# w_ada sums on TensorE beside the first z half, triangular inverses from 16-blocks, last two token quarters begun with the FFN

## Chip, cores and metric

One core of a Trainium2 chip runs the program. The metric is device time in microseconds from launch to end; a measurement of this kernel tells differences of about 0.2% apart. The kernel is written in Bass and Tile: program order gives each instruction its priority, and the Tile scheduler, which plays the program through a model of the machine, fixes the order on every engine and on each DMA queue. An engine then runs its list strictly in that order, so an instruction that waits holds everything behind it. All DMAs named below but a few at the start are issued from SP's one queue.

## What is computed

```python
c_act = silu(c)
sh_m, sc_m, g_m, sh_f, sc_f, g_f = split(c_act @ w_ada + b_ada, 6)   # w_ada: 1024 x 6144
h = modulate(rms_norm(x), sh_m, sc_m)                                # x: 1024 x 1024
proj = h @ w_in                                                      # z: 1792 columns, u: 512
z = z + mu_shift * (shifted(z) - z)
y_rwkv = rwkv7_time_mix(z, ...)        # 8 heads x 64, a recurrence over 1024 tokens
y_s5 = s5_mix(u, ...)                  # 32 groups of a 64-wide complex diagonal state, then a GLU
x = x + g_m * (concat(y_rwkv, y_s5) @ w_out)
h = modulate(rms_norm(x), sh_f, sc_f)
x = x + g_f * ((silu(h @ w_gate) * (h @ w_up)) @ w_down)             # 2816 wide
return rms_norm(x) * final_gain
```

All in float32. The recurrence multiplies a 64 x 64 state per head by a decay and adds two rank-one terms per token.

## The kernel before

The tokens are taken in two halves of 512 for the projections and the FFN, and in four quarters of 256 for the recurrence. Every large product is three passes of float32r matmuls on operands split in a high and a low part (`mm3`, L266; `split`, L129): the high part is a ScalarE copy, the low part a subtraction on GpSimd or VectorE.

**The adaptive vectors.** `ada_load` (L280) fetches 128*n columns of w_ada for all 1024 rows in four DMAs. `ada_acc` (L289) multiplies the eight row blocks by the columns of `cact` and adds them up, 128 partial sums per column left on the partitions: one VectorE instruction per block (L295, L297), or a ScalarE product (L299) and a GpSimd sum (L300). `ada_cols` (L303) sums over the partitions with one matmul per 128 columns (`pac`, L306). Parts 0 and 1 are needed before anything is projected and are done at the start, four column blocks at a time. Parts 2 and 3 run beside `chains(0)` and `chains(1)` (`ada_steps`, L826, woven in L1251 and L1417), parts 4 and 5 beside the first output projection (L1428).

**The start** (to L592): x is loaded, normed, transposed and modulated to hT, u = h @ w_in is formed (`u_mm`, L365, tile `pu`), and the small S5 parameters are worked out on VectorE.

**The z halves.** `zblock` (L857, tile `pz`) forms 128 columns of z for 512 tokens with 24 matmuls, mixes in the shifted z and writes to `zt_d`. In the first half each weight block is loaded from w_in, split, and spilled as split to `zw_d` (`z_w`, L526); in the second it is read back. `zhalf(0)` is woven with the S5 units (L1224), `zhalf(1)` with the first two quarters.

**A quarter.** `prepare` (L1152) reads z from `zt_d` with eight DMAs and forms decays, keys and bonuses in 12 steps for each of two head groups (`prep`, L888; matmuls `pw`, `pa`, `pn`, `pb`). `post` (L1162) forms the chunk matrices `ak`, writes their strictly lower parts to `l_d`, and calls `solve` and `rest`. `solve` (L991) inverts the diagonal blocks of the 64-token triangles: it reads 32 x 32 blocks with the right-hand side's columns spread over the partitions, and substitutes in 31 steps of a product (L1006) and a sum (L1008), on VectorE for quarters 0 and 1 and on GpSimd for 2 and 3. The result and its transpose go through `x_d`. `rest` (L1013) joins two 32-inverses to one of 64 with 32 x 32 matmuls (`pG`, `pO`). `chains` (L1085) runs the four chunks of the recurrence, four steps each, and `finishes` (L1186) norms and gates the output into `y_d`.

**The order** is written out from L1220 on with `weave` (round robin over generators, with a number of steps each), `LIM` (only so many steps) and `alongside`. Around the change:

```python
1224  weave((zhalf(0), 2), LIM(s5g, 14))
1251  weave(c0, (LIM(glg, 18), 2), LIM(adg, 12))
1417  weave(LIM(c1, 14), finishes(0), (glg, 1), (adg, 3))
1425  weave(seq(c1, finishes(1)), LIM(o0, 4), LIM(late, 4))
1429  weave((LIM(late, 16), 2), o0, (LIM(adl, 2), 1))
1442  alongside(late, f0, 2)
1450  weave(LIM(f0, 28))
1451  weave((f0, 1), seq(outproj(1, ...), norm_f(1, ...)))
```

`late` (L1421) is quarters 2 and 3, 128 steps. `o0` is the output projection of the first half (`outproj`, L1282, tile `po`), 18 steps. `f0` (L1441) is the norm and the FFN of the first half, 97 steps; `alongside` (L1211) gives it one step for every two of `late`. Matmuls of the FFN are `pgate`, `pup` and `pdn`. The first 20 steps of `late` come before `f0` begins; of `f0`, 54 steps go with the rest of `late`, 28 alone, and 15 are left to run beside the second output projection.

## Time and profile before

| | |
|---|---|
| runs shown, median (lowest to highest) | 1596.32 us (1594.2 to 1597.29) |
| the profiled execution | 1596.48 us, span 1594.8 us |
| TensorE busy | 1419.0 us, 89% |
| VectorE busy | 929.3 us, 58% |
| ScalarE busy | 562.7 us, 35% |
| GpSimd busy | 519.8 us, 33% |
| mean granted TensorE clock | 0.946 of 2.4 GHz |
| moved by DMA | 211.8 MB, 133 GB/s over the span |

The busy share of the whole span says little here, since the stages have different limits. The windows of the trace cut the span by stage: the start (to 104 us), the first z half (to 226 us), the second with quarters 0 and 1 (to 444 us), the remaining chains with the GLU and the first output projection (to 670 us), the FFN of the first half with quarters 2 and 3 (to 1106 us), the second output projection and norm (to 1240 us), the FFN of the second half. For each engine a window has the busy time and in brackets the number of instructions; matmuls are pipelined, so their busy time contains waits inside a burst. The granted clock is given as a share of 2.4 GHz; its two levels are 1.2 and 2.4 GHz. The chain of waits goes back from the end of a stretch, at each step to what released it last.

### The profile page before, as it was taken

How to read it: one execution, taken by the hardware profiler on the slowest of the kernel's cores; microseconds unless marked ns; L12 is line 12 of the kernel's file. 1: busy time of each engine (PE TensorE's matmuls, PEld its weight loads, DVE VectorE, ACT ScalarE, POOL GpSimd, SP SyncE). 2: the span in 40 equal slices, each digit the busy share in tenths (PEclk: the TensorE clock that was granted, in tenths of full speed). 3: DMA queues.
4: the chain of work that ended last, by engine and by line, in shares of the span. 5: the costliest groups of instructions: out<-in, count | busy, mean ns of one | idle time of the engine just before them, and what ended most of it. 6: DMA issues, size and time to landing. Idle time of an engine off the chain costs nothing.

```text
span 1594.8 us, 23226 instructions
## 1 busy us (share of the span) xinstructions
PE 1419.0 (89%) x9167; PEld 1143.2 (72%) x9167; DVE 929.3 (58%) x1618; ACT 562.7 (35%) x909; POOL 519.8 (33%) x480
## 2 busy tenths in 40 slices
PE   3897888988968847989999998999997999999997
PEld 3675666776856535777777776778886888888885
DVE  5968328688656899464467655446356533333335
ACT  4442244443345632242145223224444222222223
POOL 4358333222143415163000007000611244444543
PEclk9998899899979869899999999899998999999999
DMA  9447895563664477244233243315621423232331
GB/s 286 139 139 244 264 328 193 164 163 110 154 160 125 126 219 217 59 103 97 61 99 91 88 106 89 84 54 167 177 80 40 151 87 106 92 106 92 98 101 53
DMA packets 255692, 211.80 MB, mean 133 GB/s; under 512 B 71894, under 2 KB 223072, under 8 KB 252000
## 3 DMA queue, kind: packets, MB, share of 16 engines
q1 hardware_dynamic: 254096, 208.67, 44.0%
q8 instruction: 72, 1.18, 0.3%
q0 software_dynamic: 816, 0.57, 0.2%
q10 hardware_dynamic: 672, 1.08, 0.2%
q14 instruction: 36, 0.29, 0.1%
HBM read 166.54 MB, written 45.84 MB: 133 GB/s over the span
## 4 chain that ended last, share of the span: by engine, by line
PE 51%; DVE 19%; DMA 13%; POOL 5%; ACT 5%; issue 4%; SPq 2%; DVEq 0%; ACTq 0%; POOLq 0%
PE pdn L270 11%; PE pgate L270 10%; PE pup L270 10%; PE pz L270 5%; PE po L1314 4%; DMA wada<-in_w_ada_dram 3%; PE pu L367 2%; DMA rawd<-in_ffn_w_down_dram 2%; PE p L1062 2%; DVE acc L297 2%; POOL stmp L1006 2%; POOL XU L1008 2%; PE pY L762 1%; PE pA L962 1%; DMA LU<-l_d 1%
## 5 line engine op out<-in xcount | busy, mean ns | idle before, releaser
L270 PE MATMUL pdn<-wd,act 128*128 128x512 f32 x1056 | 271.7, 398 | 1.4 <-DVE x L1363 0.5
L270 PE MATMUL pup<-h,hl_up 128*128 128x512 f32 x1056 | 266.5, 395 | 0.2 <-ACT hl_up L131 0.2
L270 PE MATMUL pgate<-h,hl_g 128*128 128x512 f32 x1056 | 262.7, 394 | 2.1 <-ACT hl_g L131 2.0
L270 PEld LDWEIGHTS pdn<-wd,act 128*128 128x128 f32 x1056 | 197.3, 189 | 49.1 <-DVE x L1363 2.4
L270 PEld LDWEIGHTS pgate<-h,hl_g 128*128 128x128 f32 x1056 | 196.6, 188 | 47.2 <-issue 3.2
L270 PEld LDWEIGHTS pup<-h,hl_up 128*128 128x128 f32 x1056 | 197.5, 188 | 43.9 <-issue 2.1
L270 PE MATMUL pz<-hT,hl_z 128*128 128x256 f32 (+1 forms) x1008 | 192.6, 347 | 35.0 <-ACT zo L872 13.5
L1363 DVE TENSOR_TENSOR x<-pdn,x 128x512 f32<-128x512 f32 x176 | 118.8, 688 | 176.6 <-PE pdn L270 176.4
L270 PEld LDWEIGHTS pz<-hT,hl_z 128*128 128x128 f32 x1008 | 159.0, 206 | 64.8 <-ACT zo L872 18.2
L1398 DVE TENSOR_TENSOR rawd<-rawd,gfb 128x1024 f32<-128x1024 f32 x44 | 57.2, 1300 | 111.5 <-DMA rawd<-in_ffn_w_down_dram 89.9
L1314 PE MATMUL po<-wo,yhl 128*128 128x512 f32 x384 | 98.7, 410 | 9.0 <-ACT yhl L1299 4.2
L1314 PEld LDWEIGHTS po<-wo,yhl 128*128 128x128 f32 x384 | 74.4, 197 | 27.3 <-ACT yhl L1299 4.3
L131 ACT CAST wd<-rawd 128x1024 fp32r<-128x1024 f32 x44 | 45.6, 1051 | 122.1 <-DVE rawd L1398 88.8
L131 ACT CAST hl_up<-raw_up 128x1024 fp32r<-128x1024 f32 x44 | 46.2, 1051 | 114.6 <-PE pup L270 105.1
L297 DVE SCALAR_TENSOR_TENSOR acc<-wada,cact,acc 128x256 f32<-128x256 f32 (+1 forms) x112 | 79.0, 710 | 6.9 <-DMA wada<-in_w_ada_dram 5.3
L875 POOL TENSOR_TENSOR zo<-zo,zm 128x512 f32<-128x512 f32 x28 | 44.2, 1580 | 99.5 <-ACT zo L872 86.6
L127 POOL TENSOR_TENSOR hl_g<-raw_g,hl_g 128x1024 fp32r<-128x1024 f32 x19 | 45.5, 2394 | 78.7 <-ACT hl_g L131 78.7
L127 POOL TENSOR_TENSOR yhl<-yt,yhl 128x512 fp32r<-128x512 f32 x16 | 25.0, 1562 | 135.5 <-ACT yhl L1299 130.9
L1392 ACT ACTIVATE sgt<-pgate 128x512 f32<-128x512 f32 x44 | 26.3, 599 | 121.0 <-PE pgate L270 120.0
L127 POOL TENSOR_TENSOR wd<-rawd,wd 128x1024 fp32r<-128x1024 f32 x19 | 49.7, 2616 | 57.4 <-ACT wd L131 57.4
L127 POOL TENSOR_TENSOR wo<-wraw,wo 128x512 fp32r<-128x512 f32 x32 | 44.4, 1393 | 73.6 <-ACT wo L131 73.6
L127 POOL TENSOR_TENSOR hl_up<-raw_up,hl_up 128x1024 fp32r<-128x1024 f32 x19 | 49.9, 2628 | 50.0 <-ACT hl_up L131 50.0
(373 smaller groups left out, 2345.5 us busy)
## 6 DMA issues: line engine op xcount, KB each, us to landing
raw_g<-in_ffn_w_gate_dram SPq DMA_DIRECT2D x44, 512.0 KB, 4.0
raw_up<-in_ffn_w_up_dram SPq DMA_DIRECT2D x44, 512.0 KB, 3.9
rawd<-in_ffn_w_down_dram SPq DMA_DIRECT2D x44, 512.0 KB, 3.6
wada<-in_w_ada_dram SPq DMA_DIRECT2D x64, 256.0 KB, 3.2
zw_d<-hl_z SPq DMA_DIRECT2D x14, 1024.0 KB
hl_z<-zw_d SPq DMA_DIRECT2D x14, 1024.0 KB, 4.9
wada<-in_w_ada_dram SPq DMA_DIRECT2D x16, 512.0 KB, 7.8
wraw<-in_w_out_dram SPq DMA_DIRECT2D x32, 256.0 KB, 4.4
```

The costliest lines, as they stand in the source:

```text
L127: (eng or G).tensor_tensor(out=out, in0=a, in1=b, op=ALU.subtract)
L131: S.copy(dst[:, 0], src)
L270: PE.matmul(ps, lhsT=lf(a, k), rhs=rf(b, k), start=(n == 0), stop=(n == 3 * kb - 1))
L297: V.scalar_tensor_tensor(out=acc, in0=wt, scalar=cact[:, k:k + 1], in1=acc, op0=ALU.mult, op1=ALU.add)
L367: PE.matmul(pu[hf, b], lhsT=uw[b][:, a_, k, :], rhs=hT[hf, k][:, b_, :], start=(k == 0 and n == 0), stop=(k == 7 and n == 2))
L875: G.tensor_tensor(out=o, in0=o, in1=zm[:, 0:HT], op=ALU.add)
L1006: SOLVE.tensor_tensor(out=t, in0=LU[:, j, j + 1:32].unsqueeze(2).to_broadcast([P, nt, nk]), in1=X[:, j:j + 1, 0:nk].to_broadcast([P, nt, n ...
L1008: SOLVE.tensor_tensor(out=X[:, j + 1:32, 0:nk], in0=X[:, j + 1:32, 0:nk], in1=t, op=ALU.add)
L1062: PE.matmul(ps[r, h], lhsT=a, rhs=b, start=(n == 0), stop=(n == len(ops) - 1))
L1314: PE.matmul(pss[i], lhsT=yh[k][:, a, 128 * i:128 * i + 128], rhs=wo[:, b], start=(k == 4 and n == 0), stop=(k == 3 and n == 2))
L1363: V.tensor_tensor(out=t, in0=ps, in1=t, op=ALU.add)
L1398: V.tensor_tensor(out=raw, in0=raw, in1=gfb, op=ALU.mult)
```

## The change

1. `ada_acc` multiplies on TensorE. `cz` holds each column of `cact` in a block of 32 columns of which the other 31 are zero; the eight row blocks are eight float32 matmuls with 32 weight columns each, spread over four column groups of the array (`tile_position`), two row blocks accumulated in each. ScalarE copies the four times 32 rows from PSUM, and `ada_cols` sums them as before.
2. `ada_steps` runs all of parts 2 to 5 beside `zhalf(0)`, three steps a round, with eight buffers for the loads, the sums one load behind and the column sums one behind these, in PSUM banks `c0` and `c1`. The two later places go.
3. `solve` inverts 16 x 16 blocks in 15 steps on VectorE in every quarter. `rest` joins two of them to 32 with three groups of 64 matmuls of 32 x 32 and three VectorE operations. `x_d` is one buffer for all quarters, zeroed once; each quarter writes its 16-blocks in four DMAs and reads it back in two.
4. `late` no longer starts beside the chains and the output projection; all 128 steps go with `f0`, so that 64 of its steps run with them, 28 alone, and 5 are left.

```diff
@@ -157,6 +157,14 @@
+    mlow = const.tile([P, 32], F32, name="mlow")
+    V.memset(mlow, 0.0)
+    for b in range(4):
+        G.affine_select(
+            out=mlow[32 * b:32 * b + 32, 0:16], in_=mlow[32 * b:32 * b + 32, 0:16], pattern=[[0, 16]], base=16,
+            channel_multiplier=-1, compare_op=ALU.is_gt, fill=1.0,
+        )
@@ -215,6 +223,8 @@
+    cz = const.tile([P, 8, 32], F32, name="cz")
@@ -238,7 +248,7 @@
-    x_d = dram.tile([4, 2, 65536], F32, name="x_d")
+    x_d = dram.tile([2, P, HT], F32, name="x_d")
@@ -286,18 +296,14 @@
-    def ada_acc(pl, wts, n, eng=V):
-        acc = pl.tile([P, 128 * n], F32, tag="acc", bufs=2 if n > 2 else 3, name="acc")
+    def ada_acc(pl, wts, n, ps):
         for k in range(8):
-            wt = wts[k // 2][:, k % 2, :]
-            if k == 0:
-                V.tensor_scalar_mul(acc, wt, cact[:, 0:1])
-            elif eng is V:
-                V.scalar_tensor_tensor(out=acc, in0=wt, scalar=cact[:, k:k + 1], in1=acc, op0=ALU.mult, op1=ALU.add)
-            else:
-                S.mul(wt, wt, cact[:, k:k + 1])
-                G.tensor_tensor(out=acc, in0=acc, in1=wt, op=ALU.add)
+            g = slice(32 * (k % 4), 32 * (k % 4) + 32)
+            PE.matmul(ps[g, 0:128 * n], lhsT=cz[:, k, :], rhs=wts[k // 2][:, k % 2, :], start=(k < 4), stop=(k > 3),
+                      tile_position=(0, 32 * (k % 4)))
+        acc = pl.tile([P, 128 * n], F32, tag="acc", bufs=2, name="acc")
+        S.copy(acc, ps[:, 0:128 * n])
@@ -316,6 +322,8 @@
+    V.memset(cz, 0.0)
+    V.tensor_copy(cz[:, :, 0], cact)
@@ -537,7 +545,7 @@
-    acs = [ada_acc(sp, w, 4) for w in wa]
+    acs = [ada_acc(sp, w, 4, pst.tile([P, 512], F32, tag="tp", bufs=3, name="pada")) for w in wa]
@@ -674,6 +682,10 @@
+    zero = pp.tile([P, HT], F32, name="zero")
+    G.memset(zero, 0.0)
+    for n in range(2):
+        nc.gpsimd.dma_start(x_d[n], zero)
@@ -823,20 +835,28 @@
-    def ada_steps(pl, parts, ps, mix=lambda j: j % 4):
-        todo = []
+    def ada_steps(pl, parts, ps):
+        loads, todo = [], []
+        def acc():
+            w, part, j = loads.pop(0)
+            todo.append((ada_acc(pl, w, 2, ps("pada")), part, j))
         def cols():
-            acc, part, j = todo.pop(0)
-            ada_cols(acc, part, j, 2, ps("pac2")[:, 0:2])
+            a, part, j = todo.pop(0)
+            ada_cols(a, part, j, 2, ps("pac2")[:, 0:2])
         for part in parts:
             for j in (0, 2, 4, 6):
-                todo.append((ada_acc(pl, ada_load(pl, part, j, 2, 4), 2, V if mix(j) else None), part, j))
-                if len(todo) > 2:
+                loads.append((ada_load(pl, part, j, 2, 8), part, j))
+                if len(todo) > 0:
                     cols()
+                if len(loads) > 1:
+                    acc()
                 yield
-        while todo:
-            cols()
+        while loads or todo:
+            if todo:
+                cols()
+            if loads:
+                acc()
@@ -991,35 +1011,49 @@
-        LU, tmp = t_("LU", [P, 32, 32]), t_("stmp", [P, 256])
-        X, VT = (RP[0].tile([P, HT], F32, tag=nm, name=nm) for nm in ("XU", "VT"))
-        X, VT = X.rearrange("p (i k) -> p i k", k=16), VT.rearrange("p (k i) -> p k i", i=32)
-        for o in range(2):
-            nc.sync.dma_start(LU[64 * o:64 * o + 64], l_d[qt][:, 0:2048].rearrange("r (i t) -> r i t", t=64)[:, :, 0:32])
+        LU, tmp, X, VT = t_("LU", [P, 16, 16]), t_("stmp", [P, 64]), t_("X16", [P, 16, 16]), t_("V16", [P, 16, 16])
+        nc.sync.dma_start(LU, l_d[qt].rearrange("r (x n) -> (r x) n", x=2)[:, 0:1024]
+                          .rearrange("r (i t) -> r i t", t=64)[:, :, 0:16])
         G.memset(X, 0.0)
-        for o in range(2):
-            G.memset(X[64 * o:64 * o + 64].rearrange("p i k -> p (i k)")[:, 16 * o:512:33], 1.0)
-        SOLVE = V if qt < 2 else G
-        for j in range(31):
-            nt, nk = 31 - j, j // 2 + 1
+        G.memset(X.rearrange("p i k -> p (i k)")[:, 0:256:17], 1.0)
+        for j in range(15):
+            nt, nk = 15 - j, j + 1
             t = tmp[:, 0:nt * nk].rearrange("p (a b) -> p a b", b=nk)
-            SOLVE.tensor_tensor(out=t, in0=LU[:, j, j + 1:32].unsqueeze(2).to_broadcast([P, nt, nk]),
-                                in1=X[:, j:j + 1, 0:nk].to_broadcast([P, nt, nk]), op=ALU.mult)
-            SOLVE.tensor_tensor(out=X[:, j + 1:32, 0:nk], in0=X[:, j + 1:32, 0:nk], in1=t, op=ALU.add)
-        SOLVE.tensor_copy(VT.rearrange("p k i -> p i k"), X)
-        nc.sync.dma_start(x_d[qt, 0].rearrange("(r n) -> r n", r=P), X.rearrange("p i k -> p (i k)"))
-        nc.sync.dma_start(x_d[qt, 1].rearrange("(r n) -> r n", r=P), VT.rearrange("p k i -> p (k i)"))
+            V.tensor_tensor(out=t, in0=LU[:, j, j + 1:16].unsqueeze(2).to_broadcast([P, nt, nk]),
+                            in1=X[:, j:j + 1, 0:nk].to_broadcast([P, nt, nk]), op=ALU.mult)
+            V.tensor_tensor(out=X[:, j + 1:16, 0:nk], in0=X[:, j + 1:16, 0:nk], in1=t, op=ALU.add)
+        V.tensor_copy(VT.rearrange("p k i -> p i k"), X)
+        for n, w in enumerate((X, VT)):
+            d = x_d[n].rearrange("(r s) (i k) -> s r i k", s=2, k=32)
+            for s_ in range(2):
+                nc.sync.dma_start(d[s_, :, :, 16 * s_:16 * s_ + 16], w[s_::2])
     def rest(qt):
-        XB, VB, GT = (t.rearrange("p (u k) -> p u k", k=32) for t in
-                      [RP[0].tile([P, HT], F32, tag=nm, name=nm) for nm in ("XU", "VT")] + [tr("GT")])
-        for o in range(2):
-            src = x_d[qt, :, 32768 * o:32768 * o + 32768]
-            nc.sync.dma_start(XB[:, :, 16 * o:16 * o + 16], src[0].rearrange("(u p k) -> p u k", u=16, k=16))
-            nc.sync.dma_start(VB[o::2], src[1].rearrange("(u p i) -> p u i", u=16, i=32))
+        XB, VB = (t_.rearrange("p (u k) -> p u k", k=32) for t_ in
+                  [RP[0].tile([P, HT], F32, tag=nm, name=nm) for nm in ("XU", "VT")])
+        GT = tr("GT").rearrange("p (u k) -> p u k", k=32)
+        for n, w in enumerate((XB, VB)):
+            nc.sync.dma_start(w, x_d[n].rearrange("(u b) (i k) -> (b i) u k", u=16, k=32))
         aks = [sts[qt, q]["ak"] for q in range(2)]
+        def blocks(nm, lf, rf):
+            ps = ps_g(nm).rearrange("p (u k) -> p u k", k=32)
+            for u in range(16):
+                for b in range(4):
+                    r = slice(32 * b, 32 * b + 32)
+                    PE.matmul(ps[r, u, :], lhsT=lf(r, u, b), rhs=rf(r, u), start=True, stop=True,
+                              tile_position=(32 * b, 32 * b))
+            return ps
+        ps = blocks("pH", lambda r, u, b: aks[u // 8][r, u % 8, 0, 0, 32 * (b % 2):32 * (b % 2) + 32], lambda r, u: XB[r, u, :])
+        V.tensor_tensor(out=GT, in0=ps, in1=mlow.unsqueeze(1).to_broadcast([P, 16, 32]), op=ALU.mult)
+        ps = blocks("pX", lambda r, u, b: VB[r, u, :], lambda r, u: GT[r, u, :])
+        V.tensor_tensor(out=XB, in0=ps, in1=XB, op=ALU.add)
+        ps = blocks("pV", lambda r, u, b: GT[r, u, :], lambda r, u: VB[r, u, :])
+        V.tensor_tensor(out=VB, in0=ps, in1=VB, op=ALU.add)
@@ -1029,8 +1063,7 @@
-            S.copy(GT[p0:p0 + 32].rearrange("p u (k o) -> p u o k", o=2),
-                   ps[p0:p0 + 32].rearrange("p u (o k) -> p u o k", o=2))
+            S.copy(GT[p0:p0 + 32], ps[p0:p0 + 32])
@@ -1221,7 +1254,10 @@
-    weave((zhalf(0), 2), LIM(s5g, 14))
+    ads = ExitStack()
+    adg = ada_steps(pool("adp2", stack=ads), (2, 3, 4, 5), lambda nm: ps_t("c0" if nm == "pada" else "c1", nm))
+    weave((zhalf(0), 2), LIM(s5g, 14), (adg, 3))
+    ads.close()
@@ -1245,10 +1281,9 @@
-    gls, ads = ExitStack(), ExitStack()
+    gls = ExitStack()
-    adg = ada_steps(pool("adp2", stack=ads), (2, 3), ps_s)
-    weave(c0, (LIM(glg, 18), 2), LIM(adg, 12))
+    weave(c0, (LIM(glg, 18), 2))
@@ -1414,23 +1449,17 @@
-    weave(LIM(c1, 14), finishes(0), (glg, 1), (adg, 3))
-    ads.close()
+    weave(LIM(c1, 14), finishes(0), (glg, 1))
-    weave(seq(c1, finishes(1)), LIM(o0, 4), LIM(late, 4))
+    weave(seq(c1, finishes(1)), LIM(o0, 4))
-    das = ExitStack()
-    adl = ada_steps(pool("adp3", stack=das, side="right"), (4, 5), ps_a, lambda j: True)
-    weave((LIM(late, 16), 2), o0, (LIM(adl, 2), 1))
-    for _ in adl:
-        pass
+    weave(o0)
-    das.close()
```

(The second call of `ada_acc` at the start changes in the same way as the first.)

## Rows read from the trace of the kernel before

**Rows 1.** Windows by stage: us busy of PE, PEld, DVE, ACT, POOL; clock; DMA share; GB/s

```profile
0.00:104.00 104.00, 70.71 (x359) 59.62 (x359) 69.78 (x205) 47.89 (x71) 37.96 (x45) 0.93 0.63 194
104.00:226.00 122.00, 99.72 (x496) 76.74 (x496) 73.28 (x48) 34.89 (x48) 76.03 (x67) 0.87 0.78 255
226.00:444.00 218.00, 193.59 (x1734) 162.57 (x1732) 161.68 (x364) 92.65 (x177) 50.47 (x49) 0.95 0.56 166
444.00:670.00 226.00, 167.09 (x1476) 128.47 (x1474) 163.38 (x334) 97.85 (x193) 89.13 (x90) 0.83 0.53 154
670.00:1106.00 436.00, 419.69 (x3031) 330.11 (x3028) 252.75 (x394) 138.64 (x202) 75.25 (x138) 0.98 0.33 90
1106.00:1200.00 94.00, 93.79 (x420) 77.23 (x419) 39.39 (x53) 40.22 (x65) 33.01 (x24) 1.00 0.51 140
1200.00:1240.00 40.00, 30.57 (x154) 25.59 (x153) 29.16 (x45) 15.28 (x27) 6.00 (x4) 0.87 0.21 70
```

**Rows 2.** The chain of waits, 444 to 670 us, shares by line

```profile
by line: DVE acc L297 12.2%; DMA wada<-in_w_ada_dram 11.6%; PE po L1314 9.9%; issue 6.3%; DMA zz<-z_d 4.2%; DVE zz L820 2.8%; PE p L1062 2.8%; PE pglu L270 2.7%; DVE acc L295 2.5%; ACT L804 2.3%; DVE zz L805 2.2%; DVE rz L946 1.7%; DMA wraw
```

**Rows 3.** The chain of waits, 0 to 104 us: start us, us, what

```profile
36.30 6.46 DMA wada<-in_w_ada_dram
60.88 14.99 PE pu L367 x54
```

**Rows 4.** The chain of waits, 444 to 670 us: float32 matmuls, 512 and 256 columns

```profile
495.56 1.06 PE pv L1106 x2
498.69 1.06 PE pg L1121 x4
```

**Rows 5.** DMA issues, whole span: KB each, median us to landing

```profile
wada<-in_w_ada_dram SPq DMA_DIRECT2D x64, 256.0 KB, 3.2
```

**Rows 6.** Issues of line 285 on SP's queue: ns min/median/max, first and last

```profile
L285 SPq DMA_DIRECT2D wada<-in_w_ada_dram x80: 367/374/3073, 2.7 to 632.3; - x80
```

**Rows 7.** Windows of the first z half, the two with the highest rate

```profile
200.00:240.00 40.00, 33.52 (x174) 26.02 (x173) 10.41 (x16) 16.27 (x27) 14.95 (x21) 0.91 0.94 328
200.00:210.00 10.00, 8.98 (x36) 6.83 (x36) 1.23 (x1) 4.08 (x6) 4.22 (x3) 0.83 1.04 394
```

**Rows 8.** Timeline of a solve's blocks: start us, us, instruction, idle before

```profile
455.66 1.92 PE L1028 MATMUL pG<-XU,ak 32*32 32x32 f32 x64 [3.84 <-DMA XU<-x_d]
```

**Rows 9.** Timeline, TensorE from po to the 64x64 form and back

```profile
651.92 0.62 PEld L962 LDWEIGHTS pA<-ar,bk 64*64 64x64 f32 x10 [0.35 <-issue]
652.72 2.60 PEld L1314 LDWEIGHTS po<-wo,yhl 128*128 128x128 f32 x12 [0.17 <-issue]
```

**Rows 10.** Groups of instructions, whole span: the solves on VectorE

```profile
L1008 DVE TENSOR_TENSOR XU<-XU,stmp 128x126 f32<-128x126 f32 (+22 forms) x62 | 18.6, 300 | 1.3
L1006 DVE TENSOR_TENSOR stmp<-LU,XU 128x126 f32<-128x126 f32 (+22 forms) x62 | 16.4, 265 | 4.3 <-DMA LU<-l_d 2.9
```

**Rows 11.** Groups of instructions, 444 to 670 us: w_ada on VectorE and TensorE

```profile
L297 DVE SCALAR_TENSOR_TENSOR acc<-wada,cact,acc 128x256 f32<-128x256 f32 x84 | 57.2, 686 | 3.7 <-DMA wada<-in_w_ada_dram 2.4
L295 DVE TENSOR_SCALAR acc<-wada,cact 128x256 f32<-128x256 f32 x16 | 9.2, 573 | 12.3 <-POOL hl_glu L127 7.4 <-DMA wada<-in_w_ada_dram 5.0
...
L306 PE MATMUL pac<-ones,acc 128*128 128x1 f32 x64 | 10.1, 261 | 18.3 <-ACT sg L804 8.8 <-DVE acc L297 5.4 <-DVE sq L923 1.7
```

**Rows 12.** Groups of instructions, whole span: matmuls of the decay and norm steps

```profile
L921 PE MATMUL pn<-sq,blk 128*128 128x512 f32 x16 | 10.6, 747 | 2.6 <-ACT sq L919 1.8 <-ACT gmb L1265 0.7
...
L901 PE MATMUL pw<-wzk,wa 64*128 64x256 f32 x32 | 10.0, 436 | 0.6 <-DVE bo L950 0.6
```

**Rows 13.** The chain of waits, 670 to 1106 us, shares by line

```profile
by line: PE pdn L270 10.1%; DMA rawd<-in_ffn_w_down_dram 8.6%; PE pgate L270 7.8%; POOL stmp L1006 7.1%; POOL XU L1008 7.0%; PE p L1062 6.7%; PE pup L270 6.4%; issue 5.0%; DMA raw_g<-in_ffn_w_gate_dram 3.8%; DVE x L1363 2.9%; DMA LU<-l_d 2.
```

**Rows 14.** The chain of waits, 1106 to 1240 us, shares by line

```profile
by line: PE po L1314 30.6%; PE pgate L270 15.8%; PE pdn L270 13.2%; PE pup L270 12.5%; PE ptr L1340 7.0%; DMA yt<-y_d 5.9%; issue 1.9%; DVE x L1323 1.5%; DVE yo L1322 1.5%; PE pgb L1264 1.3%; POOL wo L127 1.3%; DVE wd L127 0.9%; SPq L1309 0
```

**Rows 15.** The chain of waits, 104 to 226 us, shares by line

```profile
by line: PE pz L270 24.8%; issue 13.7%; DMA raw_z<-in_w_in_dram 13.0%; DVE hl_z L127 6.8%; DMA zt_d<-zo 5.4%; DVE s5w L613 5.0%; DVE s5ca L618 4.9%; DVE s5w L616 3.3%; POOL zo L875 3.2%; POOL zlast L874 2.9%; POOL s5tw L617 2.6%; SPq L531 2
```

More of the change, by code (lines that the diff above doesn't have):

```diff
@@ L552 @@
     dgs = norm_x(1, xts[1])
-    acs = [ada_acc(sp, w, 4) for w in wa]
+    acs = [ada_acc(sp, w, 4, pst.tile([P, 512], F32, tag="tp", bufs=3, name="pada")) for w in wa]
     transpose_x(xts[1], dgs)
```

## Prediction

> **What bounds the kernel now.** I read the windows by stage first, then the chain of waits of each stage, then the groups of instructions behind the largest links. All times are of the one profiled execution, 1596.5 us with a span of 1594.8 us; the median of the runs shown is 1596.3 us, so a change of the one is read as a change of the other. In the windows [rows 1] TensorE is the limit from 670 us on: 419.7 of 436 us busy with the clock at 0.98, then 93.8 of 94. After that 1200 to 1240 us has idle time (30.6 of 40 busy). The time that is not TensorE's lies before 670 us. From 0 to 104 us it is busy for 70.7 us, from 104 to 226 us for 99.7 of 122 us at clock 0.87, from 226 to 444 us for 193.6 of 218, and from 444 to 670 us for 167.1 of 226 us at a mean clock of 0.83, the lowest of the table. So 444 to 670 us is the stage with most to give. Its chain [rows 2] says what holds it: the VectorE sums of w_ada (L297 12.2%, L295 2.5%) and the w_ada transfers (11.6%), 26.3% of 226 us or 59 us. The po matmuls, the useful work there, have 9.9%.
>
> **The change, part by part.**
>
> *w_ada off VectorE at the start (0 to 104 us).* The new mask and the padded copy of c are made while the first transfers are under way, and cost nothing. In the chain [rows 3] a w_ada transfer holds the stage until 42.8 us, and the 54 pu matmuls that then run without a gap begin at 60.9 us. In the 18 us between, VectorE does the last sums, mixed with other small work. TensorE has little to do then, and takes the sums: 32 matmuls of 128x512. The transfers stay, so at most these 18 us go. What remains of them is the modulation, behind which the matmuls wait. I take -12 us, between -18 and +5 (the sums become matmuls ahead of pu in one queue; serial they are 32 x 0.53 = 17 us [rows 4], and the stage has 33 us of idle TensorE).
>
> *The other four parts moved beside the first z half (104 to 226 us).* The move brings 64 transfers of 256 KB [rows 5], 16.8 MB, with 0.37 us of issue on SP's queue each [rows 6], 24 us of SP in 122. SP is the only queue of the z weights, the z spills and the z results too; a w_ada load that waits for one of its eight buffers stops all these behind it. The stage moves 255 GB/s now, 31.1 MB [rows 1]. With 16.8 MB more it is 47.9 MB. The best 40 us stretch moved 328 GB/s, the best 10 us 394 GB/s [rows 7]. At 328 the stage takes 146 us, 24 us more; at 394 GB/s 122 us, no more; at today's 255 GB/s 188 us, 66 more. I take the rate held for 40 us, less a few us for loads that slip into the next stage, where the DMA share is 0.56: +20 us, from 0 to +66.
> The Trainium skill ("DMA: Bandwidth & Descriptors", Specifications) gives about 358 GB/s as the share of one core; by that figure it would be 134 us, an estimate of +12 us. The 394 GB/s of [rows 7] goes above it for 10 us, so here the trace decides.
> TensorE's part: 128 matmuls of 128x256 with 32-column weights. The nearest full-width form takes 1.06 us for four [rows 4], so 34 us if they run one after the other, and a quarter, 8.5 us, if the four column groups run side by side, as the 32x32 blocks do (64 in 1.92 us, 30 ns each [rows 8]). 99.7 + 34 is 134 us, under the 146 us of the transfers, so it costs nothing as long as they are the limit; with faster transfers it is up to +12 us. Each switch between a full and a tiled form shows 0.35 us of idle before the tiled one and 0.17 us after it [rows 9]. 20 groups of sums make 10 us more of TensorE, under the same cover, and the 12 groups of blocks below 6 us, half of it in a stage that is full.
> The Trainium skill ("TensorEngine Tiling (Array Packing)", Tiling Modes) says that changing the tiling mode drains the engine; [rows 9] agree in kind and set the price.
> ScalarE evacuates each sum, 20 copies beside 34.9 of 122 us busy, and the zero fill of x_d is a memset and two transfers on GpSimd, busy 76 of 122 us [rows 1]: nothing, unless GpSimd's own S5 work comes to be the last.
>
> *Inverses from 16-blocks (226 to 444 us: quarters 0 and 1).* The old solves are 62 + 62 VectorE instructions, 16.4 + 18.6 = 35.0 us [rows 10]. The new ones are 30 steps per quarter on at most 64 elements; below the means of 265 and 300 ns, which hold for up to 126 elements and more, I take 0.2 us, 6 us per quarter. Added: 192 block matmuls of 30 ns per quarter in three groups, 5.8 us, and three VectorE operations of some 0.7 us. x_d is now written in pieces of 64 bytes instead of 2 KB, and one buffer serves all quarters, so the next quarter's write waits for the last one's read. On the chain that is 17.5 us less and 6 + 5.8 + 2 + some 3 us more per quarter, almost nothing; on TensorE, busy 89% there, it is up to 11.5 us more. I take +3, from -19 (the blocks fall into idle time and x_d stays as quick) to +14.
>
> *444 to 670 us.* Away go the 84 sums and 16 first products on VectorE, 66.4 us of its 163.4 [rows 1, 11], the ScalarE and GpSimd shares of the same, the 64 loads, and the first 20 steps of the third quarter. One end: TensorE keeps 167 us of busy time at clock 0.83, less 10 us of column sums [rows 11] and as much for the moved steps; 147 us are 122 at full clock, so -104 with no idle time left. The other end: only the two VectorE links of [rows 2], 14.7% or 33 us, come back and something else fills the waits. The 59 us of [rows 2] is the direct reading, and the moved steps are late on the same VectorE. I take -75. Next in line there are the chains of the second quarter, the GLU and ScalarE's table changes.
>
> *670 us on.* The 20 moved steps issue pn, pb, pw and pa matmuls: pn 10.6 and pw 10.0 us for four quarters [rows 12], the other two about as much, so 10 for one, busy times that overlap others and are partly of a low clock: 6. Their eight loads from zt_d pass on SP from the w_out loads to the FFN weights, where the DMA share is 0.33, and their VectorE and ScalarE work goes where both have room (252.8 and 138.6 of 436 us): nothing. The blocks of quarters 2 and 3 add 11.5 us. TensorE is full, so both count, 17 us. In return the GpSimd solves leave a path on which they have 14.1% of 436 us, 61 us [rows 13]; almost all of that is covered by FFN matmuls, and only the stage's 16 us of idle can come back. I take 5 of them: +12, from -10 to +25.
>
> *1106 to 1240 us.* Here the rest of the first FFN half fills the second output projection: pgate, pdn and pup are 41.5% of 134 us [rows 14], 56 us. After the change, 64 instead of 54 FFN steps have gone with the late quarters, so 5 instead of 15 are left. The work is only moved, but the waits are bare: the y load (5.9%, 7.9 us), the evacuation between the halves (yo and x, 3.0%, 4 us). I take +10, from 0 to +35.
>
> Sum: -12 + 20 + 3 - 75 + 12 + 10 = -42 us: 1596.5 - 42 = 1554 us.
>
> **Rivals.**
> *Queue (slower).* The z half does not hold 328 GB/s, since z weights queue on SP behind w_ada loads that wait for buffers. At 255 GB/s that is +66 instead of +20, and with the 444 us stage at the direct 59 us: -12 + 66 + 3 - 59 + 12 + 10 = +20, 1616 us. With the rest as forecast it turns the sign at 47.9 MB / (122 + 62) us = 260 GB/s. For it: raw_z transfers are already 13.0% of that stage's chain [rows 15]. Against: 40 us of it went at 328 GB/s.
> *Other waits take over (no change).* From 444 us on only the 33 us of VectorE come back: -12 + 20 + 3 - 33 + 12 + 10 = 0, 1596 us. For it: many small links in [rows 2]. Against: VectorE loses 40% of its work there.
> *Cover runs out.* The late quarters outlast the first FFN half, so their end and all of the projection stand bare: +35 and +25 for the last two terms, 1592 us. Against: the late solves shrink from 30 us [rows 13] to some 17 us each.
> *The loads fit and the stage empties.* The z half takes its loads at 394 GB/s (0), the 444 us stage falls to within 8 us of its floor (-96), the last two terms are +5 each: -95, 1502 us.
> *The loads do not come in the z half* but slip past it (their buffers lie where the S5 parameters stood): the z half costs +5, the next stage +10: -47, 1549 us, the forecast's time for another reason.
>
> **Numbers.** The forecast, and the slipped loads, which come to the same: 0.60 (1530 to 1580 us). Fits and empties: 0.10. Other waits: 0.12, about its middle. Cover: 0.05. Queue: 0.13. A measurement of this kernel tells 0.2%, 3.2 us. Faster: 0.60 + 0.10, 0.05 of the other waits, 0.03 of the cover, 0.78. Slower: 0.13 + 0.04 of the other waits, 0.17. Same: the remaining 0.05. The range leaves out half of the fourth rival and most of the queue: 1505 to 1605 us.
>
> **What would show it.** Right: no w_ada transfer after the first z half; that half some 20 us longer at over 300 GB/s; the stage from the second z half's end to the first FFN matmuls near 150 us; no L1006 or L1008 work on GpSimd. Wrong: raw_z or w_ada transfers that hold the z half beyond 170 us; a stage after it still above 190 us; TensorE idle for over 30 us around the second output projection.

## The result and the profile after

The changed kernel takes 1658.8 us (median of 4 runs, 1657.1 to 1660.3), the kernel before 1596.8 us beside it: ratio 1.0379, 95% interval [1.0352, 1.0407], slower by 62 us. The forecast was 1554.

The windows by stage of the changed kernel, at its own boundaries (first z block, its halves' ends, first FFN half, last y_d write, second FFN half), against [rows 1]:

```profile
0.00:102.00 102.00, 83.64 (x424) 57.63 (x424) 43.68 (x174) 51.30 (x75) 37.92 (x50) 1.00 0.69 210
102.00:223.00 121.00, 95.85 (x496) 75.58 (x496) 68.00 (x43) 34.60 (x48) 74.89 (x67) 0.89 0.73 247
223.00:436.00 213.00, 195.69 (x1480) 153.62 (x1480) 102.05 (x182) 74.44 (x144) 47.52 (x45) 0.94 0.70 231
436.00:722.00 286.00, 218.06 (x2795) 169.35 (x2793) 171.92 (x386) 117.07 (x226) 71.06 (x71) 0.80 0.29 78
722.00:1194.00 472.00, 465.60 (x3976) 365.29 (x3976) 285.88 (x480) 147.28 (x221) 3.72 (x6) 1.00 0.32 87
1194.00:1270.00 76.00, 57.88 (x234) 46.41 (x235) 19.22 (x41) 25.03 (x46) 31.54 (x24) 0.80 0.43 124
1270.00:1656.00 386.00, 374.05 (x1624) 300.71 (x1622) 158.42 (x198) 103.05 (x139) 158.20 (x67) 0.99 0.31 94
```

The first z half is as long as before and moves 247 GB/s, no more than the 255 of [rows 1]: the w_ada loads are not in it. The DMA share has gone up in the next row (0.70 for 0.56). The stage from the second z half's end to the first FFN half, forecast near 150 us, has 286, with TensorE idle for 68 of them and at clock 0.80. From 1194 us on the second output projection stands bare: 57.9 of 76 us busy. VectorE and GpSimd did lose work (the whole-span sums fall from 929 to 849 and from 520 to 425 us); it was not what the path waited for.

The w_ada loads and the first zt_d load of quarter 0, by tile, in the changed kernel (ns min/median/max, first and last start):

```profile
L295 SPq DMA_DIRECT2D wada<-in_w_ada_dram x64: 367/384/1974, 221.0 to 336.0; - x64
...
L902 SPq DMA_DIRECT2D wz<-zt_d x4: 336/410/522, 348.4 to 478.6; - x4
```

and that zt_d load in the kernel before:

```profile
L882 SPq DMA_DIRECT2D wz<-zt_d x4: 320/382/462, 226.5 to 370.7; - x4
```

All 64 loads issue at the end of the z half (its last matmul ends at 222.9 us) or after it, and quarter 0 begins 122 us later than it did. The built program's SBUF addresses give a reason why the loads come late, which e1 tests: the pool of the moved loads has bytes 128,192 to 146,624 of each partition, and the S5 parameters' s5w and s5tw have 123,456 to 149,056. The last reader of s5w, in the changed kernel:

```profile
L679 PE MATMUL pbt<-ident,s5w x32: 270/273/448, 172.1 to 212.1; 128*128 128x128 f32 x32
```

Quarter 0's pools (130,624 to 172,704) lie over the loads' pool in turn, and SP's waits from 330 to 360 us have one of its zt_d loads wait for the column sum of a w_ada accumulator. The wait is short, since the fixed order of SP's queue has these loads behind the last w_ada load (336.0 us) already:

```profile
SPq L902 <- PE pac L312: 1.7, 1, 1.7
```

### The profile page after: what moved, and what is told of

The parts are those of the page before. It is cut to its first block, busy times and chain, and to the rows that moved or that the text cites. A ratio compares the mean times of both kernels' runs of the same rounds, so it can differ in the third digit from the quotient of the medians.

```text
span 1656.2 us, 26614 instructions
## 1 busy us (share of the span) xinstructions
PE 1490.8 (90%) x11023; PEld 1168.6 (71%) x11023; DVE 849.2 (51%) x1499; ACT 552.8 (33%) x896; POOL 424.8 (26%) x329
## 4 chain that ended last, share of the span: by engine, by line
PE 64%; DVE 15%; DMA 9%; ACT 5%; issue 4%; POOL 1%; SPq 1%; ACTq 0%; DVEq 0%; POOLq 0%
PE pgate L280 14%; PE pup L280 14%; PE pdn L280 13%; PE pz L280 4%; PE po L1349 3%; PE p L1095 3%; PE pu L375 3%; PE pA L982 1%; PE pada L303 1%; DMA yt<-y_d 1%; DMA wada<-in_w_ada_dram 1%; PE ptr L1375 1%; PE pY L774 1%; PE pglu L280 1%; DMA wraw<-in_w_out_dram 1%
## 5 line engine op out<-in xcount | busy, mean ns | idle before, releaser
L131 ACT CAST wd<-rawd 128x1024 fp32r<-128x1024 f32 x44 | 45.7, 1050 | 126.5 <-DVE rawd L1433 94.5
L891 ACT ACTIVATE zm<-pz,cols 128x256 f32<-128x256 f32 (+1 forms) x42 | 22.9, 546 | 139.2 <-PE pz L280 135.0
L127 POOL TENSOR_TENSOR hl_g<-raw_g,hl_g 128x1024 fp32r<-128x1024 f32 x19 | 45.7, 2405 | 82.4 <-ACT hl_g L131 73.6
L131 ACT CAST hl_g<-raw_g 128x1024 fp32r<-128x1024 f32 x44 | 46.0, 1045 | 37.2 <-DMA raw_g<-in_ffn_w_gate_dram 37.2
```

The source lines that it names most:

```text
L127: (eng or G).tensor_tensor(out=out, in0=a, in1=b, op=ALU.subtract)
L131: S.copy(dst[:, 0], src)
L891: S.mul(zm[:, 1 + c0:1 + c0 + NZ], ps, col("mu", i))
```

## Experiments

A table first, since every run is read in three parts: from launch to the first gate matmul of the first FFN half, from there to that of the second half, and the rest (one profiled run each; the ratio is to the kernel before on the same chip). Each edit lets the scheduler lay all lists anew, so that a stage can also change where the edit adds nothing.

```
run                       median  ratio [95%]               to 1st half  1st half  rest
before                    1596.8  -                              694.2     522.6  378.0
changed                   1658.8  1.0379 [1.0352, 1.0407]        722.3     547.2  386.7
e1  loads' memory free    1607.5  1.0088 [1.0054, 1.0121]        689.7     526.9  386.8
e2  late alone            1625.8  1.0203 [1.0171, 1.0235]        684.3     561.3  378.0
e3  inverse alone         1631.4  1.0235 [1.0208, 1.0261]        715.1     526.7  387.1
e4  sums alone            1588.6  0.9959 [0.9938, 0.9981]        675.7     530.0  378.0
e5  128 bytes             1599.0  1.0034 [1.0009, 1.0059]        689.1     519.1  386.8
e6  inverse, late qtrs    1593.8  0.9985 [0.9960, 1.0011]        695.4     522.1  377.8
e7  sums moved alone      1589.4  0.9962 [0.9939, 0.9984]        691.3     521.9  377.8
e8  changed, mended       1603.0  1.0042 [1.0018, 1.0067]        675.9     541.0  377.8
e9  changed, old inverse  1666.0  1.0430 [1.0400, 1.0459]        725.2     558.6  377.9
e10 changed, late before  1653.6  1.0336 [1.0300, 1.0372]        737.4     527.5  386.8
e11 inverse, 256 bytes    1625.4  1.0175 [1.0143, 1.0207]        717.4     527.5  378.3
e12 sums + late inverse   1595.7  0.9993 [0.9976, 1.0011]        695.3     519.0  378.0
e13 sums alone, half      1586.8  0.9950 [0.9929, 0.9971]        673.5     529.1  377.8
e14 e1, half              1612.8  1.0110 [1.0082, 1.0138]        681.2     545.2  386.7
e15 e11 off VectorE       1605.6  1.0065 [1.0043, 1.0087]        700.3     525.6  377.9
e16 two parts moved       1600.0  1.0022 [1.0004, 1.0039]        693.2     532.3  377.9
e17 two parts, woven      1595.9  1.0001 [0.9984, 1.0019]        686.5     530.6  377.7
e18 sums alone, woven     1596.8  1.0004 [0.9985, 1.0023]        686.6     530.8  377.8
```

**e1: memory for the moved loads.**

```diff
+    adp = pool("adp2", side="right", stack=ads)
     pp = pool("pp", stack=pps, side="right")
...
-    adg = ada_steps(pool("adp2", stack=ads), (2, 3, 4, 5), ...
+    adg = ada_steps(adp, (2, 3, 4, 5), ...
```

> The changed kernel with one edit: the pool of the moved w_ada loads is opened before the pool of the S5 parameters, so that its bytes no longer lie over s5w and s5tw, which are read up to 212 us. Theory Place: in the changed kernel the 64 loads waited for those bytes (first issue 221 us, after the z half), so their sums fell into the second z half and pushed quarters 0 and 1 back by some 60 to 100 us; here the loads issue from about 105 us on, the first z half ends near 240 (20 later), the first inverse leaves for DRAM near 410 to 430 us in place of 465, and the kernel takes 1615 to 1645. Theory Late (the cost is the late quarters' start): the loads move but the time stays within 8 us of 1659.

Better than either range. The w_ada loads of e1 from 110 us on, by tile (eight more issue between 102.5 and 110 us):

```profile
L295 SPq DMA_DIRECT2D wada<-in_w_ada_dram x56: 367/435/3306, 114.0 to 249.4; - x56
```

Its windows, to be held against the changed kernel's second to fourth:

```profile
102.00:243.00 141.00, 120.65 (x760) 86.05 (x760) 59.08 (x62) 41.44 (x64) 71.87 (x66) 0.93 0.96 321
243.00:276.00 33.00, 25.21 (x139) 16.93 (x138) 17.88 (x33) 6.99 (x13) 8.86 (x10) 0.69 0.60 221
276.00:497.00 221.00, 194.54 (x2424) 163.91 (x2426) 136.94 (x291) 80.46 (x161) 39.69 (x43) 0.94 0.48 139
497.00:690.00 193.00, 160.35 (x1573) 125.95 (x1570) 120.26 (x234) 95.52 (x181) 71.68 (x65) 0.92 0.33 96
```

The z half now does what the prediction said: 141 us, 18 to 20 longer, at 321 GB/s. But 33 us follow in which the last sums and the first S5 convolutions run at clock 0.69 before the second z half begins; quarter 0's first load still issues only at 274.9 us, with the last column sum. The stage after is 193 us. One edit of a pool's place is worth 51 us between the medians (46 by the two ratios); in the profiled runs 33 us come ahead of the first FFN half and 20 in it.

**e2, e3, e4: each part alone, in the kernel before.** e2 drops `LIM(late, 4)` and `(LIM(late, 16), 2)` from the two weaves around o0; e3 takes over mlow, solve, rest and x_d; e4 takes over cz and ada_acc, with parts 2 to 5 at their old places.

> The kernel before with one part of the change: the 20 steps of the last two quarters beside the first output projection are begun with the first FFN half. Theory Late: the late quarters end some 30 to 45 us later (1135 to 1150 in place of 1105.5), the second output projection stands without FFN beside it, and the kernel takes 1615 to 1635; the stage up to the first FFN half gets shorter by 10 us at most. Theory Place: the first FFN half starts as much earlier as the late quarters lose, and the kernel stays at 1590 to 1605.

> The kernel before with one part of the change: inverses from 16-blocks, all else as before. The prediction's step: the inverse is 25 to 40 us shorter for each quarter, the three extra groups of 32x32 matmuls cost 12 to 28 us of it again, and off the path it is worth -20 to +5: 1576 to 1601. Rival (the extra groups and the DRAM writes in pieces are a wait in each quarter's chain): 1605 to 1625.

> The kernel before with one part of the change: all w_ada sums on TensorE, but parts 2 and 3 beside the chains and 4 and 5 beside the first output projection, as before. The prediction's step (VectorE freed in the stage from 444 to 670 shortens it): 1560 to 1585. Rival (the sums' float32 matmuls and the wait for loads cost on TensorE what VectorE saves): 1590 to 1610.

e2 is Late's: first FFN half 10 us earlier and 39 longer, last y_d at 1170 us (later still than expected). e3 is slower than both its ranges: 21 us ahead of the first FFN half and 9 us behind the start of the second, where none of the change's code runs. e4 lies between its two: with the sums on TensorE the first FFN half starts 18 us earlier, and 7 us of that are left in the median.

**e5, e11: 128 bytes.** The last column of the table has two values only, 378 and 387, whatever else differs; 387 goes with mlow as a tile of 128 bytes.

```diff
+    pad = const.tile([P, 32], F32, name="pad")      # e5, in before
+    V.memset(pad, 0.0)
...
-    mlow = const.tile([P, 32], F32, name="mlow")    # e11, in e3
+    mlow = const.tile([P, 64], F32, name="mlow")[:, 0:32]
```

> The kernel before with one unused tile of 128 bytes per partition where the changed kernel has its mask mlow; no instruction that matters is added, only the addresses behind it shift by 128 bytes. Theory Address (the second FFN half runs slower in the kernels that have mlow, since its weights then lie 128 bytes off in phase from the activations, which do not shift): the second FFN half from its first pdn to its last takes 352.9 us in place of 344.4, and the kernel 1601 to 1607. Rival (the block matmuls or the longer program make it slower): 344.4 us and 1591 to 1599.

> The run of the 16-block inverses alone, with the mask's tile 256 bytes in place of 128, so that the addresses keep their phase. The second FFN half takes 344.4 us; theory Queue of VectorE in quarters 0 and 1: the first FFN half still starts near 715, and the kernel takes 1615 to 1626. Rival (the address was most of it): 1595 to 1610.

200 us of the second FFN half, full of 512-column matmuls, in the kernel before, the changed one, e5 and e11:

```profile
1300.00:1500.00 200.00, 200.00 (x884) 165.60 (x883) 71.82 (x86) 51.24 (x62) 91.82 (x38) 1.00 0.33 99
```

```profile
1340.00:1540.00 200.00, 200.00 (x862) 161.47 (x861) 71.94 (x84) 48.92 (x60) 91.51 (x36) 1.00 0.32 95
```

```profile
1300.00:1500.00 200.00, 200.00 (x862) 161.49 (x861) 70.70 (x83) 50.06 (x60) 90.89 (x36) 1.00 0.31 95
```

```profile
1300.00:1500.00 200.00, 200.00 (x884) 165.61 (x883) 73.18 (x86) 49.35 (x60) 93.34 (x37) 1.00 0.32 96
```

884 or 862 matmuls at the same clock and 100% busy: an unused tile makes the half 9 us longer, 256 bytes make it whole. That half is Address's (352.9 us from its first pdn to its last in e5, 344.4 in the kernel before). In e5's profiled run the rest of the kernel came out 9 us shorter; its median is 3 us up, below the 1601 to 1607 expected and at the upper end of the rival's range. e11's total is Queue's.

**e6, e15: where the inverse's 21 us are.** e6 gives quarters 0 and 1 their old inverses (`(solve32 if qt < 2 else solve)(qt)`, the same for rest), with the mask of 256 bytes; e15 has the new ones in all four and takes the steps between the block groups off VectorE:

```diff
-        V.tensor_tensor(out=XB, in0=ps, in1=XB, op=ALU.add)
+        S.copy(hs, ps)
+        G.tensor_tensor(out=XB, in0=hs, in1=XB, op=ALU.add)
```

> The kernel before with 16-block inverses in quarters 2 and 3 only (0 and 1 keep theirs), and a mask of 256 bytes in place of 128. Theory Queue of VectorE (the 36 us of the inverse alone are 21 us of chain steps that stand on VectorE behind the three waits for block groups in quarters 0 and 1, 8.5 us of address phase and some 4 us of blocks): the first FFN half starts at 690 to 698 us as before, and the kernel takes 1588 to 1601. Rival (the blocks cost TensorE about the same in every quarter): 1606 to 1620.

> The run of the 16-block inverses with the mask of 256 bytes (1625), with the three evacuations between the block groups taken off VectorE: ScalarE copies each group to SBUF and GpSimd multiplies or adds there. Theory Queue of VectorE (chain steps stand behind the three waits): VectorE's steps of the first quarter's chain go on while the blocks wait, the first FFN half starts by 695 to 708 in place of 717, and the kernel takes 1600 to 1614, less what the two engines add. Rival (the wait is TensorE's own: the block groups stand behind z matmuls in its queue and what follows is late by that): 1617 to 1632, first FFN half at 712 or later.

Both are Queue's. Between e6 and e11, which differ in the inverses of quarters 0 and 1 alone, lie 32 us; e15 wins 20 of them back with the same matmuls on TensorE. The other 12 are not explained. What VectorE does there, in the timeline of e3:

```profile
444.47 0.29 DVE L1095 COPY U<-p 128x128 f32<-128x128 f32 x1 [2.17 <-PE p L1086]
452.03 0.69 DVE L1043 TENSOR_TENSOR GT<-pH,mlow 128x512 f32<-128x512 f32 x1 [7.26 <-PE pH L1038]
461.51 0.69 DVE L1045 TENSOR_TENSOR XU<-pX,XU 128x512 f32<-128x512 f32 x1 [8.79 <-PE pX L1038]
467.33 0.69 DVE L1047 TENSOR_TENSOR VT<-pV,VT 128x512 f32<-128x512 f32 x1 [5.13 <-PE pV L1038]
...
468.68 0.28 DVE L1099 TENSOR_TENSOR ST<-p,ST 128x128 f32<-128x128 f32 x1
```

and TensorE, in the same timeline:

```profile
444.94 0.69 PE L1038 MATMUL pH<-XU,ak 32*32 32x32 f32 x56 [0.28 <-DMA XU<-x_d]
445.55 3.13 PE L277 MATMUL pz<-hT,hl_z 128*128 128x256 f32 x24
448.61 0.69 PE L1038 MATMUL pH<-XU,ak 32*32 32x32 f32 x57
...
452.71 0.31 PE L1086 MATMUL p<-U,tm 64*64 64x64 f32 x1
452.95 3.98 PE L277 MATMUL pz<-hT,hl_z 128*128 128x256 f32 x24
456.86 0.97 PE L1038 MATMUL pX<-GT,VT 32*32 32x32 f32 x90
457.86 3.14 PE L277 MATMUL pz<-hT,hl_z 128*128 128x256 f32 x24
```

A block group of 1.3 us is cut by z blocks of 3 to 4 us, VectorE stands 7.3 + 8.8 + 5.1 = 21.2 us at the head of its queue for the three groups of quarter 1, and the state step ST of quarter 0's chain, whose last matmul ends at 453.0 us, stands behind them until 468.7. For quarter 0 the same three waits come to 3.4 us.

**e7, e8: the move, and the changed kernel mended.** e7 is e1 with the old inverses and late steps; e8 is e1 with the mask of 256 bytes and the old inverses in quarters 0 and 1.

> The changed kernel with the memory of the moved loads free, the inverses of before and the late quarters begun as before: the w_ada sums on TensorE and their move into the first z half are what is left of the change. If the parts add up (inverse 21 + 8.5 before the second FFN half and in it, late quarters hidden either way), 1568 to 1588 with the first z half at 240 to 247 us. Rival Bare sums (on TensorE the sums cost in the z half what the later stage wins): 1589 to 1603, no better than the sums left in their old places (1588.6).

> The changed kernel with three edits: the memory of the moved loads free, the mask 256 bytes, and 16-block inverses in quarters 2 and 3 only. If memory, address and VectorE's queue are what the change lost: 1607 - 21 - 8.5 = about 1577, 1568 to 1586, and the first FFN half starts at 664 to 676 us. Rival (the late start of quarters 2 and 3 comes back as a cost once the stage before it is shorter, as in the run of that part alone): 1588 to 1605.

Both are the rivals', e7 by 0.4 us. Moved with free memory, the sums are worth what they are worth at their old places (1589.4 and 1588.6). e8 gets its early first FFN half (675.9 us), and the late start takes it back (541 us for it, where kernels with the old start have 519 to 532; e1 has 527, and in it the scheduler itself listed quarter 2's first steps ahead, its l_d write at 671.6 us in place of 757.5). This order divides all kernels: where quarter 2's first l_d write comes ahead of the first gate matmul, the first FFN half takes 519 to 532 us (15 kernels); where it comes 27 to 41 us behind it (the changed kernel, e2, e8, e9, e14), 541 to 561.

**e9, e10: undone in the changed kernel.**

> The changed kernel with the inverses of before (and so without the mask of 128 bytes); the loads stay held until 221 us and the late quarters begin with the FFN. If the inverse costs here what it cost alone (36 us): 1615 to 1630. Rival (here quarters 0 and 1 run when the second z half is over, so its block groups are not kept waiting by z matmuls; only the address, 8.5 us, and the blocks' own 13 us of TensorE come back, and the old inverses of quarters 2 and 3 on GpSimd make the late quarters longer): 1636 to 1660.

> The changed kernel with the 20 steps of the late quarters beside the first output projection, as before. If the late start costs what it cost alone (31 us): 1622 to 1636, with the last y_d near 1160 in place of 1194. Rival Work (TensorE has 65 us more work at full clock than before; moving steps from one full stage to another gives none of it back): 1648 to 1662.

e9 is slower than the changed kernel and than both of its ranges: here the new inverses win 7 us, most of it in the first FFN half (558.6 us in e9, 547.2 in the changed kernel), and lose 9 by the address. The late quarters have only the FFN beside them there, and each takes 40 to 42 us from the load of LU to the write of x_d, with the new ones 16 to 20. e10 has Work's time, though the last y_d comes at 1159 us: the steps cost the stage ahead (737 us) what they spare the FFN half.

**e12: the two harmless parts together.**

> The kernel before with the two parts that cost nothing alone: w_ada sums on TensorE at their old places (1588.6 alone) and 16-block inverses in quarters 2 and 3 only (1593.8 alone), mask of 256 bytes. If they add: 1582 to 1591, the first of these kernels below before by more than 0.4%. Rival (both put work on a TensorE that is full after 670 us, and take their gain from the same waits): 1588 to 1600.

They do not add: the rival's time. Its reason is not shown, though. What e12 lacks against e4 is lost ahead of the first FFN half, which starts at 695.3 us in place of 675.7, while ahead of it the two differ only in the mask and the zero fill of x_d. The nearest reading is that an order laid anew can move that start by some 20 us; no run shows it by itself.

**e13, e14: half of the products.** `for k in range(4)` in ada_acc, in e4 and in e1.

> The run of the sums on TensorE at their old places, with only the first four of the eight products of each sum (the other half of w_ada is loaded and left out, so this output is not the reference's): 80 matmuls of 160 go, some 23 us of TensorE busy time, and nothing else. Theory Work (what the sums cost on TensorE is paid in the span, nearly one for one): 1564 to 1576. Rival Waits (the stages with the sums have idle TensorE time that takes them for nothing): 1583 to 1592.

> The changed kernel with the memory of the moved loads free, again with half of the products of each sum left out (80 matmuls of 160, some 23 us busy; this output is not the reference's). Theory Work: 1607 - 23 to 1607 - 14, 1583 to 1594. Rival Waits (the first z half is held by its transfers, whose 16.8 MB are all still there, and the sums lie beside them): 1600 to 1609.

Theory Work falls. Busy time weighted with the granted clock (summed from 10 us windows) is 1360.8 us before and 1426.3 us in the changed kernel, and I had taken these 65 us for the loss; but half of the sums gone changes the time by -2 and +5 us. e13 is in its rival's range; e14 lies above both. In e14 the first FFN half does start 8.5 us earlier and then takes 18 us more, since quarter 2's l_d write now comes behind its start (709.8 us). So it is e13 that shows the sums to lie under waits.

**e16, e17, e18: can half of the move win?** e16 moves parts 2 and 3 only (`ada_steps(adp, (2, 3), ...)` over free memory), in the kernel with old inverses and late steps; e17 and e18 replace `(LIM(adl, 2), 1)` by `(adl, 1)` in e16 and in e4.

> The changed kernel with the inverses and the late quarters as before, and only parts 2 and 3 of w_ada moved into the first z half, their pool over free memory; parts 4 and 5 are summed on TensorE beside the first output projection, as before. Theory Memory (what the move of four parts costs is that the pools of quarter 0 lie over the buffers of the moved loads, so that its first load waits for the last sum: 348 us in the changed kernel, 274 to 282 with the memory of the loads free, 222 with the sums at their old places): here the 32 loads end before the z half does, quarter 0's first load issues by 240 us, the first FFN half starts at 655 to 674 us, and the kernel takes 1566 to 1586. Rival Other waits (the stage before the first FFN half is a chain that the w_ada sums do not set): 1585 to 1595, no better than the sums at their old places (1588.6).

> The run with parts 2 and 3 moved, with the sums of parts 4 and 5 woven step by step into the first output projection; in that run six of their eight groups stood bare behind it, 638 to 667 us, 4.9 us each, and held the first FFN half at 693 us. Here three are left. Theory Bare tail: the first FFN half starts at 674 to 682 us and the kernel takes 1580 to 1592. Rival (the chain up to the projection sets it, not the tail): 688 us or later, 1594 to 1603.

> The run of the sums on TensorE at their old places (1588.6), with the sums of parts 4 and 5 woven into the first output projection: two groups bare behind it in place of three. Theory Bare tail: 3 to 6 us less, 1581 to 1586, the best of these kernels. Rival: no difference, 1587 to 1591.

e16 misses both ranges on the slow side. Quarter 0 does begin at 221 us, as Memory had it, and the first FFN half still starts at 693 us. e17's first FFN half starts 7 us earlier, not the 11 to 19 of Bare tail, and its time is the rival's; e18 loses 8 to e4, against both of its theories. So the stage ahead of the first FFN half moves by some 10 us with the order in which the same sums are listed, and what sets it stays open. No kernel tried that forms all the products is better than e4, 0.4% below before.

## Why the prediction was wrong

The stages of before, of the changed kernel and of e8, from the same marks (last u matmul, last matmul of each z half, first gate matmul of each FFN half, end), profiled runs in us; the forecast took the third mark's stage to 670:

```
stage                     forecast   before   changed        e8
start                        -12      103.3    100.8   -2.5   100.1   -3.2
first z half                 +20      123.1    122.1   -1.0   142.3  +19.2
second z half (inverses)      +3      217.1    213.3   -3.8   240.2  +23.1
to the first FFN half        -75      250.7    286.1  +35.4   193.3  -57.4
first FFN half, projection   +22      522.6    547.2  +24.6   541.0  +18.4
second FFN half                0      378.0    386.7   +8.7   377.8   -0.2
sum                          -42     1594.8   1656.2  +61.4  1594.7   -0.1
```

*Start, -12: wrong.* The sums left VectorE (69.8 to 43.7 us busy), TensorE's clock rose from 0.93 to 1.00, and 2.5 us came of it; among all runs the start ends between 100 and 105 us. In the changed kernel the chain of waits of this stage is nearly all TensorE's own from 39.2 us on (the w_ada matmuls are 6.8% of the 102 us), so there was no longer a wait for VectorE to take away.

*First z half, +20: right in size, wrong in place.* With memory free it is +18 to +20 at 321 GB/s (328 assumed). By the figure of the Trainium skill ("DMA: Bandwidth & Descriptors", Specifications), about 358 GB/s for one core, the 45 MB of that half would take 126 us, an estimate; e1 took 141.

*The step that failed* is that the loads run in that half. The prediction named the way in which they would not (their buffers lie where the S5 parameters stood) and priced it at +5 and +10, a total of 1549. It stopped at the loads: it did not ask which pools lie over the loads' own buffers. Those of quarter 0 do, so that a hold of some 115 us (first issue at 221.0, in e16 at 105.8) became a delay of 122 us of quarter 0 and of the stage behind. Price: e9 and e8, which up to the first FFN half differ in hardly more than that, reach it at 725.2 and 675.9 us, 49 us apart; the changed kernel and e1 are 33 us apart there and 51 in total time. That is half of the miss: the result lies 105 us above the forecast, and e1 still 53.

*To the first FFN half, -75: the second step that failed, wrong even with the memory mended.* In e8 it is -57, but 23 us of that were only pushed into the second z half, which was forecast at +3, and the 193 us left are above the 190 that the prediction named as a sign of being wrong. The move with free memory and nothing else is e7: -6.5 us, where the prediction's terms for it, -12 + 20 - 75, come to -67 (10 of the 75 are the late steps, by e2). The direct part, VectorE's sums gone, is e4: its first FFN half starts 18.5 us earlier, where the chain [rows 2] gave these sums 33. Even of the 18.5 only 4.3 lie in this stage; 11.1 lie in the second z half, before the first load of these parts issues (442.7 us), and e12 has none of them. The other 59 - 33 us, the w_ada transfers, do not come back by moving: e7 is no faster than e4. A line's share of a chain is what it holds while all else stays; with it gone, the chain of waits of the changed kernel from 436 to 722 us has many others in its place, none above the projection's own matmuls:

```profile
by line: PE po L1349 12.2%; PE pglu L280 4.7%; issue 4.5%; DMA yt<-y_d 4.0%; PE p L1095 3.7%; DVE X L1024 3.2%; PE ptr L1375 2.7%; DMA y_d<-zz 2.5%; DMA raw_glu<-in_s_w_glu_dram 2.4%; DVE stmp L1022 2.2%; DMA x_d<-X 1.9%; PE pA L982 1.8%; D
```

*Inverses, +3: right only beside the rest of the change.* Alone they are +36, in the profiled run +34: 21 ahead of the first FFN half, 9 of address, 4 in the first half. The durations were about right (groups of instructions of the changed kernel, busy us and mean ns as in [rows 10]; 18.2 us for four quarters, 23 forecast):

```profile
L1047 PE MATMUL pH<-XU,ak 32*32 32x32 f32 x512 | 7.0, 212 | 5.3 <-DMA XU<-x_d 5.3
L1047 PE MATMUL pX<-GT,VT 32*32 32x32 f32 x512 | 5.8, 204 | 6.1 <-DVE GT L1052 6.1
L1047 PE MATMUL pV<-VT,GT 32*32 32x32 f32 x512 | 5.4, 193 | 1.2 <-issue 1.2
```

What was left out is three waits of VectorE for TensorE and what stands behind them. In the changed kernel quarter 0 is so late that no z matmul is left to cut the groups (the last ends at 436.2 us, the first group begins at 472.9), and the 21 us are not there. That the stage came near its +3 is luck.

*First FFN half and second projection, +12 and +10: right in sum by luck, by other parts.* The late start costs 39 us with the old inverses (e2), the new ones give 20 back (e2 to e8), and 6 of the changed kernel's 25 belong to neither. In kind that is the rival Cover runs out, which had a chance of 0.05: the late quarters end at 1194 us, 3 us after the first FFN half's last matmul, and the projection is bare. Its price was not paid: +60 for the two terms, where +25 were measured. No term of the sum said when the late quarters end.

*Second FFN half: 9 us that no term had.*

The sums on TensorE, costed at nothing beside the transfers, were right: 45.7 us busy (17 and 8.5 to 34 us forecast), and leaving half of them out (e13) changes the time by 2 us, less than its interval. Their group in the changed kernel:

```profile
L303 PE MATMUL pada<-wada,cz 128*32 128x256 f32 (+1 forms) x320 | 45.7, 445 | 6.3 <-DVE cz L326 4.2 <-DMA wada<-in_w_ada_dram 1.9
```

## To carry to other kernels

Before a load is moved forward, look up whose bytes its buffers get, until when they are read, and who gets them next: program order put the loads into the z half, the memory put them behind it, and the quarters behind the loads. A new round trip between two engines is priced by what stands behind its waits in the in-order queue, not by its instructions. And a part that gains alone may gain nothing beside another: parts that cost +31, +36 and -7 us alone came to +62 with the move, of which one pool's place was about 50.

## What the runs showed that was not expected

A tile of 128 bytes that nothing reads costs 9 us: in the second FFN half 200 us hold 862 of the 512-column matmuls in place of 884, one in 232 ns in place of 226, and the 9 us are there in each kernel that has such a tile (6 of 6) and in none without (14 of 14). By the built program's addresses the tile moves the FFN weights by 128 bytes, while the input activations of the second half, allocated from the other end, stay; those of the first half move along, and that half keeps its pace. Shifts of 256, 1024 and 1280 bytes do nothing. That it is the phase of the two operands modulo 256 bytes fits all of these, but no run moved the activations.

A float32 matmul leaves two records where the three-pass ones leave one: the 8 pn calls are the x16 of [rows 12]. The prediction took the two records of [rows 4] for two matmuls of 0.53 us, where they are one of 1.06; the prices of the sums and blocks held all the same, by luck. The sums, 32 of 1.06 and 128 of 0.53 us one after the other, would be 102 us and were 45.7, as the four column groups ran partly side by side. The 64 records of [rows 8] are 32 matmuls, 60 ns each at clock 0.53 (455 to 458 us); the new groups took 18.2 us for 768, 24 ns each.
